# Low-rank products of the decays and rates on 64 rows of the array each, both directions side by side, in place of 128 rows with zeros

## The chip, the cores and the metric

The kernel runs on one core of a Trainium2 chip. A core has five engines with a queue of instructions each: TensorE (PE in the profile, with weight loads as PEld) for matrix products, VectorE (DVE), ScalarE (ACT), GpSimd (POOL) and SyncE (SP), which here issues the transfers between the core's memory and HBM. Each queue runs in order; an instruction waits on semaphores for what it needs. The metric is the device time of one execution in microseconds.

## The reference, cut to what matters

The program is two blocks, one after the other. The first (two layers of sparse attention, convolution and pooling) is not touched. Each of the two layers of the second computes an attention (`_mla`) and a bidirectional recurrence (`_rwkv_bidir`) from one projection, mixes them, and ends with a mixture of experts. The change is in the recurrence, 512 channels wide and 528 positions long, and there in the two products `tanh(wd) @ w2[d]` (decays) and `ad @ a2[d]` (rates), whose inner dimension is 64:

```python
r, k, v, wd_f, wd_b, ad_f, ad_b, gd = _split(u, [RW, RW, RW, 64, 64, 64, 64, 128])
...
def direction(d, wd, ad, reverse):
    wl = w0[d] + jnp.tanh(wd) @ w2[d]
    decay = jnp.exp(-jnp.exp(-jax.nn.softplus(-wl) - 0.5))
    a = jax.nn.sigmoid(a0[d] + ad @ a2[d])
    kd = heads(k * (1.0 + (a - 1.0) * k_a))
    y = _wkv_scan(rh, heads(decay), kd, vh, kk, heads(a), reverse)
    bonus = jnp.sum(rh * kd * r_k, -1, keepdims=True) * vh
    return y, bonus

y_f, bonus_f = direction(0, wd_f, ad_f, False)
y_b, bonus_b = direction(1, wd_b, ad_b, True)
```

## The kernel before, in words

Everything of the second block lies with channels on the 128 partitions and the 528 positions along the free dimension. A product over all positions is made in two halves of 264 (`HALF`), each in a PSUM tile of its own; the pool `ps` has four such tiles. A 32-bit product shows as two matmul instructions in the trace.

`mixers` runs one layer of the second block's first part (about 880 to 1400 us and 1885 to 2400 us of the span). It first makes some projections (`shifted`, which calls `proj_tile`, line 1029). The projections number 12 and 13 are the inputs of the low-rank products: `low[0]` has tanh of the decays' 64 channels of direction 0 in rows 0 to 63 and those of direction 1 in rows 64 to 127; `low[1]` has the same for the rates.

The 512 channels are then worked in four pairs of heads, 128 channels each, by four generators of `rwkv_pair`. `mixers` advances them by turns, by the rules of `RULES`, and between their steps it takes from `fill`, a generator with all other work of the layer: the other projections, the attention, the output. A pair's first steps are named "go", the later ones "invert", "double" and "chain" (short products of 64 columns). In which order instructions then stand on each engine is decided by a scheduler, from the order in which the code issues them and from when tiles come free.

In the "go" steps a pair does the following, first for direction 0 and then for direction 1. It makes the decays (`w0`) and rates (`a0`) with products over `wl` (line 1431, which calls the helper `halves`, line 994); ACT evacuates each half with a tanh (1433); POOL scales the decays (1437); DVE scans them over time (1439 or 1441); POOL, ACT and DVE make the exponentials and the scaled keys from them (1442 to 1456); POOL scales chunks of the keys (1464). Behind the second direction POOL adds the two directions' keys (1469), DVE multiplies that with the receptance (1471), and TensorE sums it over channels for the bonus (1472, again line 994).

The weight tile `wl` (one buffer) has, for each kind and each direction, 128 rows, of which only 64 are filled: the rest is set to zero by POOL (1382), and four transfers (1385) bring 64 rows each. So a product runs over all 128 rows of `low`, and the rows of the other direction meet zeros.

Weights of `fill`'s projections come by transfer (1017) into `big`, and are split into two parts by ACT (932) and POOL (933); `big` has 22 buffers, `u` has 10, and both are shared with `rwkv_pair`.

Of the kernel before, what the change touches and what calls it, by code (L numbers as in the profile page):

```python
# [12 lines left out]
AF = mybir.ActivationFunctionType  # L13
# [9 lines left out]
HALF = 264  # L23
# [169 lines left out]
class K:  # L193
# [1181 lines left out]
    def rwkv_pair(self, l, i, low, v2, vlow, yd):  # L1375

        nc, A = self.nc, self.A
        cs = slice(i * 128, (i + 1) * 128)
        idc = self.c("ident")

        wl = self.t("wl", [128, 2, 2, 128], 1)
        nc.gpsimd.memset(wl, 0.0)
        for j, k in enumerate(("rwkv_w2", "rwkv_a2")):
            for d in range(2):
                nc.sync.dma_start(wl[d * 64:d * 64 + 64, j, d], A[k][l][d * 64:d * 64 + 64, cs])
        rk = self.big()[:, :2 * L2].rearrange("p (j t) -> p j t", j=2)
        nc.sync.dma_start(rk, self.rw[i:i + 5:4].rearrange("j p t -> p j t"))
        R, Kk = rk[:, 0], rk[:, 1]
# [7 lines left out]
        else:  # L1396
            vf, t = self.u()[:, :L2], self.u()[:, :L2]
            nc.sync.dma_start(vf, self.vfirst[i])
            ps = self.halves([v2[:, cs]], [vlow[:32]])
# [7 lines left out]
        s = self.u()[:, :L2]  # L1407
# [6 lines left out]
        kr, bk = [], []  # L1414
# [5 lines left out]
        def chunk(x, o):  # L1420

            if o is None:
                return x[:, :16]
            return x[:, 16:].rearrange("p (c n) -> p c n", n=64)[:, o::2]
        for d in range(2):
            x = self.big().rearrange("p (s n) -> p s n", s=2)
            kr.append(x)
            lw, P = x[:, 0], x[:, 1]
            a, c, kd = self.u()[:, 48:], self.u(), self.u()[:, 48:]
            for j, (dst, nm) in enumerate(((lw[:, 48:], "w0"), (a, "a0"))):  # L1430
                ps = self.halves([wl[:, j, d]], [low[j]])
                for x in range(2):
                    nc.scalar.activation(dst[:, x * HALF:(x + 1) * HALF], ps[x][:, :HALF], AF.Tanh, scale=0.5,
                                         bias=self.pc(nm, d * 4 + i, True))
            yield "go"
            nc.gpsimd.memset(lw[:, :48], 0.0)
            nc.gpsimd.tensor_scalar(lw[:, 48:], lw[:, 48:], e5, e5, op0=ALU.mult, op1=ALU.add)
            if d == 0:
# [16 lines left out]
            x = self.big().rearrange("p (c s n) -> p c s n", c=9, s=2)  # L1455
# [16 lines left out]
        ps = self.halves([self.c("ones64")], [bonus])  # L1472
        for x in range(2):
            xs = slice(x * HALF, (x + 1) * HALF)
# [5 lines left out]
        ps, p8 = self.ps(), self.ps()  # L1480
# [43 lines left out]
        for d in range(2):  # L1524
# [6 lines left out]
            for par in range(2):  # L1531
                both = [self.ps() for _ in range(2)]
                self.warm(both[1])
                for j in range(4):
                    c = 2 * j + par if d == 0 else 8 - 2 * j - par
# [4 lines left out]
                for hh, ps in enumerate(both):  # L1540
# [6 lines left out]
                    for x, G in enumerate((GA, GC)):  # L1547
# [4 lines left out]
            c = 8 if d == 0 else 0  # L1552
            ps = self.ps()
# [3 lines left out]
                             start=True, stop=True)  # L1557
# [15 lines left out]
        for part, k0 in enumerate((0, 3, 6)):  # L1573
            ps = self.ps()
# [830 lines left out]
```

## Time and profile before

| | |
|---|---|
| timed runs | 2747.86, 2748.91, 2754.46 us, median 2748.91 |
| the profiled execution | 2744.74 us, its span 2743.0 us |
| mean granted clock of TensorE | 0.928 of full speed |
| busy: PE, DVE, ACT, POOL | 2368.5, 1490.2, 910.3, 781.8 us |

The span is the time from the first to the last instruction that the profiler shows; the execution's own time is 1.7 us more. Busy times of different engines overlap. A matmul's duration in the trace holds the time until its result is there, so for instructions behind one another the distance of their starts is what each costs.

### The profile page before, as it was taken

Reading aid. Unit: us, or ns where it says so; the run is one execution under the profiler, and the core shown is the slowest. Engines: PE = TensorE matmul, PEld = TensorE weight load, DVE = VectorE, ACT = ScalarE, POOL = GpSimd, SP = SyncE. Lnnn points to the kernel's source line nnn. Section 1 sums busy time; section 2 is a strip of 40 time slices with the busy share of each in tenths; the row PEclk is TensorE's granted clock in tenths of the full one; section 3 lists DMA queues with packets and bytes.
Section 4 is the critical chain, followed back from the end, with each engine's and each line's share of the span. In section 5 each row is a group of like instructions: output and inputs, shape, how many; then the busy total and the mean of one; then the engine's idle time right before and its main releaser. Section 6 shows DMA issues by size and latency. Waiting matters only on the chain. (4 is left out here: it accounts for less than half of the span.)

```text
span 2743.0 us, 48138 instructions
## 1 busy us (share of the span) xinstructions
PE 2368.5 (86%) x19363; PEld 1846.0 (67%) x19363; DVE 1490.2 (54%) x3197; ACT 910.3 (33%) x1832; POOL 781.8 (29%) x707
## 2 busy tenths in 40 slices
PE   8988988987969879988896999779888998969994
PEld 7664887664968767666765666468766677756662
DVE  2896233995246785667536321166766675363213
ACT  3346322246243334445402111143435464021111
POOL 5634425635311640222022110035422120121102
PEclk9998999998989999989998899979899999979997
DMA  5421123411235322101216899663230113179996
GB/s 180 108 70 40 51 79 91 108 54 40 63 128 157 96 89 89 43 22 62 96 65 225 313 416 413 258 206 122 80 101 15 46 65 109 60 263 370 414 409 238
DMA packets 208611, 401.32 MB, mean 146 GB/s; under 512 B 25474, under 2 KB 129538, under 8 KB 197376
## 3 DMA queue, kind: packets, MB, share of 16 engines
q1 hardware_dynamic: 195232, 376.50, 38.7%
q0 software_dynamic: 7776, 14.30, 1.5%
q10 hardware_dynamic: 5376, 7.40, 1.1%
q8 instruction: 154, 2.52, 0.4%
q14 instruction: 73, 0.60, 0.1%
HBM read 351.83 MB, written 52.94 MB: 148 GB/s over the span
## 5 line engine op out<-in xcount | busy, mean ns | idle before, releaser
L294 POOL TENSOR_TENSOR wl<-raw,wh 128x1024 fp32r<-128x1024 f32 (+1 forms) x92 | 220.1, 2402 | 268.5 <-ACT wh L293 268.1
L1029 PE MATMUL sc<-gy,w 128*128 128x264 f32 x1216 | 224.5, 300 | 28.7 <-DVE ph L1900 11.4
L1029 PEld LDWEIGHTS sc<-gy,w 128*128 128x128 f32 x1216 | 183.6, 199 | 38.4 <-issue 13.5
L300 PE MATMUL ps<-wh,xh 128*128 128x256 f32 x640 | 188.1, 294 | 6.3 <-DVE xl L313 3.4
L300 PE MATMUL ps<-wh,xl 128*128 128x256 f32 x640 | 181.1, 283 | 2.5 <-POOL xl L709 2.1
L300 PE MATMUL ps<-wl,xh 128*128 128x256 f32 x640 | 181.4, 284 | 1.1 <-POOL wl L294 1.1
L300 PE MATMUL ps<-xh,wh 128*128 128x512 f32 (+1 forms) x400 | 166.4, 416 | 7.6 <-ACT att L458 7.6
L300 PE MATMUL ps<-xh,wl 128*128 128x512 f32 (+1 forms) x400 | 161.7, 404 | 0.1
L300 PE MATMUL ps<-xl,wh 128*128 128x512 f32 (+1 forms) x400 | 161.7, 404 | 0.0
L2307 PE MATMUL ps<-big,hTr 128*64 128x256 f32 x1200 | 158.8, 384 | 2.6 <-DMA big<-in_moe_w_dram 2.3
L293 ACT ACTIVATE wh<-raw 128x1024 fp32r<-128x1024 f32 (+1 forms) x92 | 93.4, 1029 | 169.6 <-PE ps L300 61.7
L1029 PE MATMUL sc<-big,w 128*128 128x264 f32 x608 | 134.8, 296 | 2.0 <-DVE big L933 2.0
L2307 PEld LDWEIGHTS ps<-big,hTr 128*64 128x64 f32 x1200 | 97.6, 139 | 53.7 <-issue 7.1
L300 PEld LDWEIGHTS ps<-wh,xh 128*128 128x128 f32 x640 | 122.6, 192 | 8.8 <-DVE xl L313 4.0
L526 DVE SCALAR_TENSOR_TENSOR a<-pz,ph,a 128x512 f32<-128x512 f32 x120 | 124.3, 1036 | 2.6
L300 PEld LDWEIGHTS ps<-wh,xl 128*128 128x128 f32 x640 | 122.5, 192 | 3.4 <-POOL xl L709 2.5
L300 PEld LDWEIGHTS ps<-wl,xh 128*128 128x128 f32 x640 | 122.7, 192 | 2.4 <-POOL wl L294 1.4
L2250 DVE SCALAR_TENSOR_TENSOR mh<-mh,ps 128x256 f32<-128x256 f32 x32 | 13.5, 421 | 185.0 <-ACT mh L2249 185.0
L2085 POOL DMA_INDIRECT zd<-my,idx x32 | 31.6, 989 | 271.3 <-ACT my L270 244.5
L1627 ACT ACTIVATE z<-ps,mix 128x512 f32<-128x512 f32 x144 | 77.7, 577 | 80.0 <-PE ps L1517 71.0
L1029 PEld LDWEIGHTS sc<-big,w 128*128 128x128 f32 x608 | 101.9, 199 | 3.2 <-DVE big L933 2.8
L300 PEld LDWEIGHTS ps<-xh,wh 128*128 128x128 f32 (+1 forms) x400 | 77.3, 193 | 36.1 <-ACT att L458 11.3
(497 smaller groups left out, 5896.7 us busy)
## 6 DMA issues: line engine op xcount, KB each, us to landing
big<-in_moe_w_dram SPq DMA_DIRECT2D x216, 512.0 KB
w8m<-in_moe_w_dram SPq DMA_DIRECT2D x48, 1024.0 KB
w<-in_moe_w_dram SPq DMA_DIRECT2D x36, 1024.0 KB
raw<-in_w_in_dram SPq DMA_DIRECT2D x56, 512.0 KB
big<-in_w_in_dram SPq DMA_DIRECT2D x36, 512.0 KB
raw<-in_w_out_dram SPq DMA_DIRECT2D x16, 512.0 KB
raw<-in_ple_gate_w_dram SPq DMA_DIRECT2D x16, 512.0 KB
big<-zd SPq DMA_DIRECT2D x16, 512.0 KB
```

The costliest lines, as they stand in the source:

```text
L293: nc.scalar.activation(hi[:, x:x + 4], v, AF.Copy)
L294: nc.gpsimd.tensor_tensor(lo[:, x:x + 4], v, hi[:, x:x + 4].bitcast(F32), op=ALU.subtract)
L300: self.nc.tensor.matmul(ps, a[x], b[y], start=start and j == 0, stop=stop and j == 2)
L526: nc.vector.scalar_tensor_tensor(acc, u[:, s:s + S], ph[:, tp + s:tp + s + 1], acc, op0=ALU.mult, op1=ALU.add)
L1029: self.nc.tensor.matmul(ps[x][:, :HALF], w[a][:, k], hT[k // 2][b][:, k % 2, x * HALF:(x + 1) * HALF], start=k == 0 and a == b == 0, stop= ...
L1627: nc.scalar.activation(Z[g][q][:, :self.WIDTH[g]], ps[:, :self.WIDTH[g]], AF.Copy, scale=self.c("half")[:, q:q + 1])
L2085: ins = nc.gpsimd.indirect_dma_start(out=zd[:, :], out_offset=bass.IndirectOffsetOnAxis(ap=idx[:, j, 1:2], axis=0), in_=y, in_offset=None, ...
L2250: nc.vector.scalar_tensor_tensor(a, a, 1.0, p1[:, :256], op0=ALU.add, op1=ALU.mult)
L2307: self.nc.tensor.matmul(ps[q * 64:q * 64 + 64, :256], xT[:, k, q * 64:q * 64 + 64], ww[q][k], start=k == 0, stop=k == 7)
```

## The change

`wl` loses its zeros and the dimension for the direction: 128 rows, of which rows 0 to 63 belong to direction 0 and rows 64 to 127 to direction 1. The memset is gone, and one transfer per kind brings both directions. The products of both directions are made in the first "go" step, before any other work on direction 0: for each kind and each half a product over rows 0 to 63 and one over rows 64 to 127, into two PSUM tiles, and then the two evacuations. The tile of direction 1 for the decays (`kr`) and that for the rates (`rates`) are taken in that step too. The number of steps of a pair is the same.

```diff
-        wl = self.t("wl", [128, 2, 2, 128], 1)
-        nc.gpsimd.memset(wl, 0.0)
+        wl = self.t("wl", [128, 2, 128], 1)
         for j, k in enumerate(("rwkv_w2", "rwkv_a2")):
-            for d in range(2):
-                nc.sync.dma_start(wl[d * 64:d * 64 + 64, j, d], A[k][l][d * 64:d * 64 + 64, cs])
+            nc.sync.dma_start(wl[:, j], A[k][l][:, cs])
...
+        rates = []
         for d in range(2):
-            x = self.big().rearrange("p (s n) -> p s n", s=2)
-            kr.append(x)
-            lw, P = x[:, 0], x[:, 1]
-            a, c, kd = self.u()[:, 48:], self.u(), self.u()[:, 48:]
-            for j, (dst, nm) in enumerate(((lw[:, 48:], "w0"), (a, "a0"))):
-                ps = self.halves([wl[:, j, d]], [low[j]])
-                for x in range(2):
-                    nc.scalar.activation(dst[:, x * HALF:(x + 1) * HALF], ps[x][:, :HALF], AF.Tanh, scale=0.5,
+            kr.append(self.big().rearrange("p (s n) -> p s n", s=2))
+            rates.append(self.u()[:, 48:])
+
+        for j, nm in enumerate(("w0", "a0")):
+            for x in range(2):
+                xs = slice(x * HALF, (x + 1) * HALF)
+                ps = [self.ps() for _ in range(2)]
+                for d in range(2):
+                    r = slice(d * 64, d * 64 + 64)
+                    nc.tensor.matmul(ps[d][:, :HALF], wl[r, j], low[j][r, xs], start=True, stop=True)
+                for d in range(2):
+                    nc.scalar.activation((rates[d] if j else kr[d][:, 0, 48:])[:, xs], ps[d][:, :HALF], AF.Tanh, scale=0.5,
                                          bias=self.pc(nm, d * 4 + i, True))
-            yield "go"
+        yield "go"
+        for d in range(2):
+            lw, P = kr[d][:, 0], kr[d][:, 1]
+            a, c, kd = rates[d], self.u(), self.u()[:, 48:]
+            if d:
+                yield "go"
```

Where instructions stand now is shown at three places. Lines of the changed kernel are up to 8 higher there: 1434 and 1436 are the products and their evacuations, 1445 the scaling of the decays (1437 before), 1472 that of chunks of the keys (1464), 1477 the bonus sum (1469).

TensorE, first pair of layer 1, from the last filler matmul (`sc`) ahead of the products (`ps<-u,wl`) on; before:

```order
L1029 MATMUL sc_15999<-gy_15074,w_2655_15897 128x264
L994 MATMUL ps_16063<-u_15358,wl_15958 128x264
L994 MATMUL ps_16064<-u_15358,wl_15958 128x264
L994 MATMUL ps_16069<-u_15547,wl_15958 128x264
L994 MATMUL ps_16070<-u_15547,wl_15958 128x264
L1029 MATMUL sc_16081<-gy_15068,w_2672_15995 128x264
```

and now:

```order
L1434 MATMUL ps_16048<-u_15346,wl_15946 128x264
L1434 MATMUL ps_16049<-u_15346,wl_15946 128x264
L1434 MATMUL ps_16054<-u_15346,wl_15946 128x264
L1434 MATMUL ps_16055<-u_15346,wl_15946 128x264
L1029 MATMUL sc_16078<-gy_15056,w_2672_15980 128x264
L1029 MATMUL sc_16079<-gy_15056,w_2672_15980 128x264
L1029 MATMUL sc_16078<-big_15057,w_2672_15980 128x264
L1029 MATMUL sc_16079<-big_15057,w_2672_15980 128x264
L1029 MATMUL sc_16078<-gy_15056,w_2672_15980 128x264
L1434 MATMUL ps_16060<-u_15535,wl_15946 128x264
L1434 MATMUL ps_16061<-u_15535,wl_15946 128x264
L1434 MATMUL ps_16066<-u_15535,wl_15946 128x264
```

The four products of direction 0 have become four of both directions' decays, and the four of the rates (one more stands behind the rows shown) follow five filler products later; the four of direction 1 that stood a hundred matmuls further on are gone from there.

ACT at the same place (evacuations of the products, then the splits of the filler's weights, `w<-big`); before:

```order
L1433 ACTIVATE big_16059<-ps_16063,ph_2562_15078 128x264
L1433 ACTIVATE big_16059<-ps_16064,ph_2562_15078 128x264
L1433 ACTIVATE u_16060<-ps_16069,ph_2562_15078 128x264
L1433 ACTIVATE u_16060<-ps_16070,ph_2562_15078 128x264
L932 ACTIVATE w_2688_16077<-big_16075 128x1024
L932 ACTIVATE w_2694_16158<-big_16156 128x1024
```

and now:

```order
L1436 ACTIVATE big_16044<-ps_16048,ph_2562_15066 128x264
L1436 ACTIVATE big_16046<-ps_16049,ph_2562_15066 128x264
L1436 ACTIVATE big_16044<-ps_16054,ph_2562_15066 128x264
L1436 ACTIVATE big_16046<-ps_16055,ph_2562_15066 128x264
L1436 ACTIVATE u_16045<-ps_16060,ph_2562_15066 128x264
L1436 ACTIVATE u_16047<-ps_16061,ph_2562_15066 128x264
L1436 ACTIVATE u_16045<-ps_16066,ph_2562_15066 128x264
L1436 ACTIVATE u_16047<-ps_16067,ph_2562_15066 128x264
L932 ACTIVATE w_2692_16074<-big_16072 128x1024
L932 ACTIVATE w_2700_16157<-big_16155 128x1024
```

Eight evacuations stand ahead of the two splits now, where there were four.

POOL, later in the same pair, up to the bonus sum (1469 before, 1477 now) and the weight split (933) behind it; before:

```order
L1437 TENSOR_SCALAR big_16215<-big_16215 128x528
L1382 MEMSET wl_16380 128x512
L933 TENSOR_TENSOR w_2707_16233<-big_16231,w_2707_16233 128x1024
L1393 MEMSET big_16388 128x48
L933 TENSOR_TENSOR w_2713_16315<-big_16313,w_2713_16315 128x1024
L1442 TENSOR_TENSOR big_16215<-u_16217,big_16215 128x576
L1447 TENSOR_TENSOR u_16218<-u_16218,big_15964 128x528
L1453 TENSOR_TENSOR big_16215<-big_15964,big_16215 128x528
L1454 MEMSET big_16215 128x2x48
L1469 TENSOR_TENSOR u_16062<-u_16062,u_16218 128x528
L1464 TENSOR_TENSOR big_16304<-u_16218,u_16217 128x16
L1464 TENSOR_TENSOR big_16304<-u_16218,u_16217 128x4x64 x2
```

and now:

```order
L1444 MEMSET big_16481 128x48
L933 TENSOR_TENSOR w_2713_16300<-big_16298,w_2713_16300 128x1024
L1450 TENSOR_TENSOR big_16046<-u_16214,big_16046 128x576
L933 TENSOR_TENSOR w_2731_16399<-big_16397,w_2731_16399 128x1024
L1455 TENSOR_TENSOR u_16215<-u_16215,big_15949 128x528
L1461 TENSOR_TENSOR big_16046<-big_15949,big_16046 128x528
L1462 MEMSET big_16046 128x2x48
L1472 TENSOR_TENSOR big_16289<-u_16215,u_16214 128x16
L1472 TENSOR_TENSOR big_16289<-u_16215,u_16214 128x4x64 x2
L1477 TENSOR_TENSOR u_16132<-u_16132,u_16215 128x528
```

The bonus sum has moved behind the three scalings of the second direction, one more weight split (`w_2731`, which stood behind it) is ahead of it, and the scaling of the second direction's decays and the memset of `wl` are no longer here.

## Rows read from the trace of the kernel before

**Rows 1.** Part 1 of the page: busy us, share of the span, instructions.

```profile
PE 2368.5 (86%) x19363; PEld 1846.0 (67%) x19363; DVE 1490.2 (54%) x3197; ACT 910.3 (33%) x1832; POOL 781.8 (29%) x707
```

**Rows 2.** Windows: length, busy PE, PEld, DVE, ACT, POOL; PEclk; DMA; GB/s.

```profile
880.00:1400.00 520.00, 455.09 (x4964) 362.56 (x4963) 344.04 (x790) 223.92 (x451) 144.96 (x151) 0.93 0.24 77
1885.00:2400.00 515.00, 454.50 (x4883) 366.26 (x4882) 329.20 (x760) 206.23 (x417) 135.09 (x151) 0.94 0.22 72
```

**Rows 3.** Work on `wl`; durations in ns as least/median/most, first and last start.

```profile
L994 PE MATMUL ps<-u,wl x128: 383/386/490, 884.7 to 2214.0; 128*128 128x264 f32 x128
...
L1385 SPq DMA_DIRECT2D wl<-in_rwkv_w_dram x16: 471/588/1882, 816.8 to 2110.1; - x16
...
L1382 POOL MEMSET wl<- x8: 519/522/527, 813.9 to 2109.0; 128x512 f32 x8
```

**Rows 4.** Timeline, TensorE: start, us, engine, line, tiles, rows*columns, form, count.

```profile
1885.25 1.94 PE L994 MATMUL ps<-u,wl 128*128 128x264 f32 x8
```

**Rows 5.** Timeline, TensorE, two places of the first block with 64-row matmuls.

```profile
142.88 0.39 PE L300 MATMUL ps<-xl,wh 128*128 128x512 f32 x1
143.11 0.40 PE L300 MATMUL ps<-xh,wl 128*128 128x512 f32 x1
143.44 0.49 PE L642 MATMUL pq<-a,a 64*128 64x128 f32 x4
143.86 0.50 PE L300 MATMUL ps<-xh,wh 128*128 128x512 f32 x1
...
184.57 0.70 PE L642 MATMUL pq<-a,a 64*128 64x256 f32 x4
185.20 0.50 PE L300 MATMUL ps<-xh,wh 128*128 128x512 f32 x1
```

**Rows 6.** Timeline, TensorE, a product among the chain's short ones.

```profile
1089.00 0.71 PE L994 MATMUL ps<-u,wl 128*128 128x264 f32 x2
```

**Rows 7.** Timeline, ACT, first pair of layer 1 (idle before in brackets).

```profile
1885.89 0.93 ACT L1433 ACTIVATE big<-ps,ph 128x264 f32<-128x264 f32 x2 [0.17 <-PE ps L994]
...
1887.61 1.99 ACT L932 ACTIVATE w<-big 128x1024 fp32r<-128x1024 f32 x2
...
1899.62 0.93 ACT L1433 ACTIVATE big<-ps,ph 128x264 f32<-128x264 f32 x2 [0.17 <-PE ps L994]
```

**Rows 8.** Timeline, DVE and TensorE, end of that pair's first steps.

```profile
1916.26 0.75 DVE L1471 SCALAR_TENSOR_TENSOR u<-u,pv,big 128x528 f32<-128x528 f32 x1
...
1917.07 1.25 PE L994 MATMUL ps<-u,mix 128*128 128x264 f32 x2 [4.06 <-DVE u L1471]
```

**Rows 9.** Timeline, POOL, the same pair.

```profile
1888.74 5.41 POOL L933 TENSOR_TENSOR w<-big,w 128x1024 fp32r<-128x1024 f32 x2 [0.97 <-ACT w L932]
...
1901.42 0.62 POOL L1437 TENSOR_SCALAR big<-big 128x528 f32<-128x528 f32 x1
...
1907.00 2.38 POOL L933 TENSOR_TENSOR w<-big,w 128x1024 fp32r<-128x1024 f32 x1 [1.29 <-ACT w L932]
...
1914.61 1.44 POOL L1469 TENSOR_TENSOR u<-u,u 128x528 f32<-128x528 f32 x1
1916.01 2.46 POOL L1464 TENSOR_TENSOR big<-u,u 128x16 f32<-128x16 f32 x3
```

**Rows 10.** Timeline, POOL and TensorE, second pair of layer 0.

```profile
967.32 0.78 POOL L1437 TENSOR_SCALAR big<-big 128x528 f32<-128x528 f32 x1 [1.56 <-ACT big L1433]
...
971.04 1.43 POOL L1442 TENSOR_TENSOR big<-u,big 128x576 f32<-128x576 f32 x1 [2.48 <-DVE u L1441]
...
978.31 2.68 POOL L933 TENSOR_TENSOR w<-big,w 128x1024 fp32r<-128x1024 f32 x1
...
965.47 2.14 PE L994 MATMUL ps<-u,wl 128*128 128x264 f32 x8
...
981.05 0.92 PE L1029 MATMUL sc<-gy,w 128*128 128x264 f32 x4 [3.65 <-POOL w L933]
```

**Rows 11.** Timeline, TensorE, second pair of layer 1.

```profile
1977.98 2.00 PE L994 MATMUL ps<-u,const 128*128 128x264 f32 x4 [4.38 <-ACT u L1089]
```

## The prediction

> **What bounds the kernel now.** I read the page's busy times first, then the busy time by stage, then all work on the tile of the low-rank weights, then the timelines of the places where the products stand. TensorE is busy for 86% of the span and everything else for about half or less [rows 1]. The page's chain of the end cannot be used here (it stops at the last few instructions), so what bounds a place is read from the waits on TensorE there. In the two stretches in which the changed code runs (about 880 to 1400 us and 1885 to 2400 us), TensorE is also busy for some 88% of the time [rows 2]. The idle rest is not one wait but many of 1 to 4 us, where a chain of POOL, ACT and DVE work or a weight transfer comes late. A saving on TensorE is worth its full size only where TensorE runs without gaps up to the next wait. Where it already waits, the saving turns into more waiting, and what counts is how the change moves POOL and ACT.
>
> **The products on TensorE.** There are 64 products (four per direction, half and kind: 8 pairs times 8), each of two instructions, so 128 [rows 3]. Eight in a row take 1.94 us with the last one's 0.386 us of latency [rows 3, 4]: (1.94 - 0.386) / 7 = 0.222 us from start to start, 0.444 us a product, and 64 x 0.444 = 28.4 us in all. After the change a product uses rows 0 to 63 or rows 64 to 127 of the array. Whether two such run side by side is shown by the scores of the first block, which have the same form (64 rows, 128 columns): four instructions of 256 columns, two products, start at 184.57 and are over at 185.20, so 0.63 us, where one after the other at 0.222 x 256/264 = 0.215 us they would take 0.86 [rows 5]. They do overlap, but two streams are 0.43, so 0.20 us more is spent inside the group. Its neighbours pay as well: the full-row matmul ahead of a group of such products holds TensorE for 0.33 us (143.11 to 143.44) where the same kind took 0.23 just before, and the one behind it takes 0.50 us where its kind takes 0.40 [rows 5]. So going into the 64-row form and out again costs 0.20 + 0.10 + 0.10 = 0.4 us, 0.2 us a change of form. The same shows on these very products, where two stand alone among products of another form: two instructions take 0.71 us, not 0.386 + 0.222 = 0.61 [rows 6].
>
> What follows for groups of different size: one pair of products alone between full-row work costs 0.444 + 0.4 = 0.84 us against 0.89 before, so nothing is won. Two pairs in a row cost 0.89 + 0.4 = 1.29 against 1.78.
>
> The Trainium skill (TensorEngine Tiling (Array Packing), Key Properties) says "Mode switching requires drain", which speaks against this change; the trace agrees, with the 0.1 us on either neighbour. The Trainium skill (TensorE: Matmul & The Clock Gate, Part 3: Packing small matmuls) gives a pack of such tiles the time of one matmul plus about 4 ns for each further one. By it all 32 pairs would halve, 14.2 us; by the trace's 0.2 us a change of form the sum is the smaller one that follows.
>
> In the order of the changed kernel, 27 times the two products of a pair of directions stand behind one another, and 10 products stand alone, since their two accumulators did not come free together. So 37 streams are left of 64: 37 x 0.444 = 16.4 us, 12.0 us less. Over TensorE's whole order, changes of form go from 953 to 972. Next to the products there are about 35 more; 16 fewer elsewhere come from other work standing in another order. 19 x 0.2 = 3.8 us. The most that TensorE's own work can shrink is therefore 12.0 - 3.8 = 8.2 us. If the fewer changes elsewhere are worth nothing, it is 12.0 - 7.0 = 5.0 us.
>
> **The other edits.** The memset goes: 8 x 0.52 = 4.2 us of POOL; and 16 of the 32 small transfers, 0.59 us of SP each, 9.4 us in all [rows 3]. POOL is busy for 29% and SP waits on buffers, so both are worth nothing by themselves except where POOL is the chain that is waited for (the first pairs, below). The 64 evacuations on ACT stay, 0.93 us for two [rows 7]. But all eight of a pair now come in one go, where four came early and four some 14 us later. A tile of `big` and one of `u` per pair are held longer; both pools (22 and 10 buffers) are shared with the weights of the filler work, so weights may be fetched one tile later. I take nothing for this, since the order of the fetches changes by one place only; were it a transfer late, it is one wait like the 3.65 us of [rows 10].
>
> **First pair of layer 1 (1885 to 1921 us).** Here TensorE has filler work up to about 1913 and then waits 4.06 us for the bonus, the DVE product at 1916.26 [rows 8]. DVE waits for POOL's sum at 1914.61, and POOL works through its queue almost without a gap from 1888.74 on [rows 9]. That queue sets the end, and the change makes it longer. First, ACT does eight evacuations ahead of the two weight splits instead of four, 4 x 0.46 = 1.9 us later [rows 7], and POOL's first split then starts some 1.7 us later. Then POOL's order: the bonus sum (old line 1469) now stands behind its direction's three scalings instead of ahead of them (2.46 us) and behind one more weight split (2.38 us). Against this, the rescaling of the second direction moves ahead of the splits (-0.62), the memset is gone (-0.52), and a wait of 1.29 us for a weight split on ACT is filled [rows 9]. Sum: 1.7 + 2.46 + 2.38 - 0.62 - 0.52 - 1.29 = +4.1 us. I take +4. The bounds: without the late start and with all of the wait gone it is +2.4; with the wait still there +5.4. TensorE's 0.5 to 1 us saved ahead of this place only lengthens its wait. The weight split that is pulled ahead may spare a later wait, which could give one or two of these back.
>
> **First pair of layer 0 (884 to 925 us).** The same chain ends in the same wait. It was shorter there and the added split does not stand in the way: the later ACT work (+1.9) less the memset (-0.52) and idle POOL time like the 0.97 us of [rows 9] leaves +0.5 us (0 to +1.9).
>
> **Second pairs.** In layer 0 TensorE waits 3.65 us for a weight split on POOL, which starts at 978.31 [rows 10]. POOL stood idle twice ahead of it, 1.56 us for the evacuations of direction 1 and 2.48 us for the scan behind them, and those hang on the four products at 965.47. These products now stand right behind those of the first direction, some 30 us earlier, so both idles can go; the split on ACT, which waits for its transfer, allows only part. I take -1.5 us (0 to -2.4). In layer 1 the matmuls of this pair stand ahead of a wait of 4.38 us for attention data [rows 11], which does not come earlier: -0.5 us. After such a wait TensorE's instructions also run slower for a while (four take 2.00 us at 1977.98 [rows 11], eight 1.94 in [rows 4]), so each microsecond of wait that goes or comes has some tenths with it.
>
> **Third and fourth pairs.** These lie in the chain stages, where TensorE has short products of 64 columns. Their streams shrink from 32 to 19 slots, 13 x 0.444 = 5.8 us, and about 11 changes of form more take 2.2 us back: 3.6 us. TensorE is busy there for much the same share as in the whole [rows 2] and waits in many small pieces, so I let some 70% pass: -2.5 us (0 to -3.6).
>
> **Sum.** +4 + 0.5 - 1.5 - 0.5 - 2.5 = 0.0 us. The profiled execution took 2744.74 us; the median of the timed runs is 2748.91, 4.2 us above it. I predict no change that can be measured: 2748 us on the scale of the median, with the little that other reordered work may give. A change under 0.3%, 8.2 us, can't be told from none here.
>
> **Rivals.**
> *The saving on TensorE passes in full.* For it: TensorE is the busy engine [rows 1, 2], and weight splits pulled ahead can fill gaps. The 8.2 us are then all kept, the second pairs give 2 us, and the bonus chain costs nothing in the end, since the pulled-ahead split removes a later wait of the same size: -10 us, and with the quicker running behind shorter waits up to -12, about 2737 us. Against it: waits stand behind the products in four of the eight pairs. Chance 0.27. The packing rule of the Trainium skill (TensorE: Matmul & The Clock Gate, Part 3) would put it a few us lower still.
>
> *ACT's eight evacuations in one go hold up what is behind them (slower).* The price is 1.9 us at each of 8 pairs [rows 7], 15 us, if the instruction behind them on ACT is one that TensorE waits for: weight splits in the first two pairs, evacuations of the chain in the other two. POOL's order in the first pair of layer 1 adds 2.4 us (4.1 less its late start). With half or all of the 8.2 us saved this gives +9 to +14, about 2759 us. With half saved it can be measured from 1.9 n + 2.4 - 4.1 = 8.2 on, n = 5 to 6 pairs of eight. Against it: ACT is busy for a third only. Chance 0.14.
>
> *The halves do not run side by side here*, because the two accumulators come free at different times or the two weights have to be loaded in turn. Then no stream is saved, 3.8 to 7 us of changes of form and the 4 us of the first pair come on top: +8 to +11, about 2758 us. Against it stands the overlap of 0.63 us in [rows 5], with the same form. Chance 0.06.
>
> No change: 0.53, by itself 2742 to 2755. The range that holds eight in ten reaches to the rivals on both sides: 2737 to 2758 us. Faster 0.27, same 0.53, slower 0.20.
>
> **What would show it.** Right: pairs of the new products start within about 0.01 us of each other and eight instructions end within 1.3 us; busy TensorE falls by 5 to 8 us; the wait ahead of the bonus in the first pair of layer 1 grows from 4.06 to about 8 us; the one for the weight split in the second pair of layer 0 falls to 2 us or less; windows from 1000 to 1400 and 2065 to 2300 us hold the same work 1 to 2 us earlier each. Wrong: starts 0.22 us apart; a wait of several us in the chain stages that ends on an ACT evacuation; weights fetched later; or a gain in stretches that the change does not touch, through the order.

## The result, and the profile after

The changed kernel is slower: 2765.76 us (2756.23 to 2771.45, six runs) against 2749.03 us of the kernel before (six runs), a ratio of 1.0062 with an interval of 1.0046 to 1.0079. I had predicted 2748 us with a range up to 2758. Its profiled execution took 2771.45 us at a granted clock of 0.921.

Part 1 of the page of the changed kernel answers to [rows 1], the two windows (same columns) to [rows 2]:

```profile
PE 2378.4 (86%) x19363; PEld 1844.7 (67%) x19363; DVE 1499.7 (54%) x3197; ACT 911.2 (33%) x1834; POOL 776.0 (28%) x699
```

```profile
880.00:1400.00 520.00, 452.37 (x4898) 359.73 (x4896) 338.62 (x776) 222.04 (x448) 138.45 (x147) 0.91 0.24 76
1885.00:2400.00 515.00, 440.16 (x4806) 350.76 (x4806) 337.10 (x756) 212.80 (x427) 132.47 (x148) 0.92 0.23 74
```

In the window of layer 1 TensorE was busy for 454.50 us and is busy for 440.16 now, with 77 matmuls fewer done by its end: so it waits more there, and is not held by longer work. Over the whole span its busy time rose from 2368.5 to 2378.4 us, where I had expected 5 to 8 us less; these durations hold the lower granted clock too, 0.921 against 0.928. The work on the weight tile, which answers to [rows 3]:

```profile
L1434 PE MATMUL ps<-u,wl x128: 382/383/806, 882.1 to 2209.8; 64*128 64x264 f32 x128
...
L1383 SPq DMA_DIRECT2D wl<-in_rwkv_w_dram x8: 333/358/1967, 816.1 to 2111.6; - x8
L1383 SPq DMA_DIRECT2D wl<-in_rwkv_a_dram x8: 413/430/738, 816.6 to 2112.0; - x8
```

And the products of the first pair of layer 1 on TensorE (timeline; [rows 4] is the same place before):

```profile
1895.26 1.16 PE L1434 MATMUL ps<-u,wl 64*128 64x264 f32 x8
1896.35 0.51 PE L1029 MATMUL sc<-gy,w 128*128 128x264 f32 x2
1896.69 0.41 PE L1029 MATMUL sc<-big,w 128*128 128x264 f32 x2
```

Eight take 1.16 us in place of 1.94, their starts are 7 ns apart within a pair of directions, and the filler behind them takes 0.51 us where it otherwise takes 0.41. So the halves run side by side here and the prices of the form are near those of the prediction. The Trainium skill (TensorE: Matmul & The Clock Gate, Part 3: Packing small matmuls) has about 4 ns for each further tile of a pack; the trace agrees in kind, with 7 ns, but shows the 0.1 us on the neighbour as well.

**Where the time went.** For each matmul I took its start in a trace less the start of the same matmul in the trace of before. The table gives this distance (us, + is later), the median over the matmuls that start in the 20 us from the given time of before on; "again" are second executions, "place only" is an experiment below:

```
time in before             860  1060  1180  1300  1860  1960  2060  2180  2300  2700
changed                   -2.7   0.9   3.8   7.9   9.9  13.4  14.5  17.8  23.5  25.6
changed, again            -1.9   1.1   4.0   8.0  10.1  13.6  14.5  17.8  23.5  21.6
place only, full rows     -3.2   0.0   3.2   6.6   6.3   9.4   9.6  13.7  18.6  20.3
before, again             -3.0  -6.0  -6.0  -4.4  -2.7  -6.6  -6.0  -6.1  -7.0  -9.0
```

Between 860 and 1060 stand the first and second pairs of layer 0, up to 1180 the third, up to 1300 the fourth; likewise for layer 1 up to 2060, 2180 and 2300. The last line shows what two executions of one kernel differ by: 3 to 4 us in the stages of the first pairs, 1.6 or less in those of the third and fourth. The third and fourth pairs lose 2.9 and 4.1 us in layer 0, 3.3 and 5.6 in layer 1, 15.9 us together (from distances before rounding), and the second execution repeats each within 0.1. The first two pairs lose 3.6 and 4.6 us, which the table alone could not tell from chance; the wait that is shown under e7 tells it for layer 1.

Two limits of this table. The two profiled executions lie 26.7 us apart and the medians 16.7, so its stages add up to more than the ratio says. And two executions of the kernel before are few: in the trace of e3 below, where the third and fourth pairs have the code of before, the distance goes from 0.7 at 1180 to 7.9 at 1300. There the granted clock (the eighth column) is low; e3, then the kernel before:

```profile
1300.00:1310.00 10.00, 10.00 (x84) 6.48 (x86) 5.91 (x17) 0.73 (x2) 2.12 (x1) 0.52 0.26 84
```

```profile
1300.00:1310.00 10.00, 9.86 (x170) 9.06 (x167) 7.75 (x28) 5.34 (x14) 0.00 (x0) 1.00 0.26 79
```

So a difference like the 4.1 us of the fourth pair of layer 0 can arise without the change, though the changed order repeats it; in the other three stages e3 has 0.1 us or less.

### The profile page after: what moved, and what is told of

It is laid out like the page before. It is cut to its first block, busy times and chain, and to the rows that moved or that the text cites. A ratio compares the mean times of both kernels' runs of the same rounds, so it can differ in the third digit from the quotient of the medians.

```text
span 2769.7 us, 48112 instructions
## 1 busy us (share of the span) xinstructions
PE 2378.4 (86%) x19363; PEld 1844.7 (67%) x19363; DVE 1499.7 (54%) x3197; ACT 911.2 (33%) x1834; POOL 776.0 (28%) x699
## 5 line engine op out<-in xcount | busy, mean ns | idle before, releaser
L1715 ACT ACTIVATE w<-ps 64x256 f32<-64x256 f32 x64 | 24.1, 377 | 251.4 <-PE ps L1706 239.9
```

Source lines behind the costliest of these rows:

```text
L1715: nc.scalar.activation(UV[qs, s].rearrange("p d n -> p (d n)"), pu[qs, :256], AF.Copy, scale=-1.0)
```

## The experiments

Ratios are to the kernel before on the same chip, with 95% intervals; each distance is to the trace of before, as in the table.

**e1: the rows alone.** The old order, and products over 64 rows one direction after the other.

```diff
-        wl = self.t("wl", [128, 2, 2, 128], 1)
-        nc.gpsimd.memset(wl, 0.0)
+        wl = self.t("wl", [128, 2, 128], 1)
...
-                ps = self.halves([wl[:, j, d]], [low[j]])
+                r = slice(d * 64, d * 64 + 64)
+                ps = self.halves([wl[r, j]], [low[j][r]])
```

> The products use 64 rows each (no zeros, no memset, one transfer per kind), but stay where they stood before, four per direction, so that none runs beside another; the order on TensorE and ACT is that of the kernel before. If the lost time comes from the form (43 changes of form more, 0.2 us each, nothing saved): 5 to 9 us slower than before. If it comes from where the products and their evacuations stand: within 4 us of before.

2759.61 us against 2747.68, 1.0037 (1.0022 to 1.0053), with TensorE and ACT in the same order as before. So the form by itself, with nothing side by side, costs 10 us by the ratio, 12 by the medians. It is not spread over the 64 products: up to 1200 us the distance is 0.4, and at 1220 it is 7.8. This place comes back under e15 and e14.

**e2: the place alone.** The changed order, with full rows and zeros as before.

```diff
-                    r = slice(d * 64, d * 64 + 64)
-                    nc.tensor.matmul(ps[d][:, :HALF], wl[r, j], low[j][r, xs], start=True, stop=True)
+                    nc.tensor.matmul(ps[d][:, :HALF], wl[:, j, d], low[j][:, xs], start=True, stop=True)
```

> The products keep 128 rows with zeros, but those of both directions are made in the first step, in the order of the change; the order on ACT is that of the changed kernel, and on TensorE too. If the place is the cause: as slow as the changed kernel or more, 15 to 24 us over the kernel before, since the 12 us of streams that run side by side are missing. If the form is the cause: within 4 us of before.

2763.69 us, 1.0064 (1.0046 to 1.0082): all of the loss, with no 64-row product in the kernel. Its line in the table loses 3.2, 3.4, 4.1 and 4.9 us in the third and fourth pairs, 15.6 together. The place is the main cause. What the form gains and costs inside this order cancels, within the intervals. Nor is it the granted clock: the mean of e2's runs is 0.925, that of the runs of the kernel before beside them 0.924.

**e3 and e4: the change for the first two pairs of each layer alone, and for the last two alone** (`i < 2` or `i >= 2` chooses the new code, otherwise the old).

> The whole change for the first two pairs of each layer only, the other two as before. If the time is lost in the chain stages of pairs three and four (15 of the 25 us that the two traces lie apart): 4 to 9 us slower than before, most of it in the first pair of layer 1, whose bonus chain comes 4 us later. If the loss is spread over all pairs alike: 8 to 9 us.

> The whole change for the third and fourth pairs of each layer only. If the time is lost in the chain stages: 8 to 16 us slower than before, and the first pairs run as before. If it was lost by what the first pairs shift: within 4 us of before, or faster by the 3 us of streams that run side by side.

2755.23 us, 1.0024 (1.0008 to 1.004), and 2758.48 us, 1.0039 (1.0021 to 1.0056): 7.6 and 10.8 us, which add up to about the whole. Both halves of the change lose, by the medians the last two pairs more (the intervals overlap), where I had expected a gain of 2.5 us. The trace of e3 has +2.6 us in the first two pairs of layer 0 and +4.4 in those of layer 1, near the changed kernel's.

**e5: the tile of direction 1 taken late.** As the changed kernel, but direction 1's tile of `big` is taken only at its turn; its decays are evacuated into a tile of `u` until then.

```diff
-            kr.append(self.big().rearrange("p (s n) -> p s n", s=2))
+            if d == 0:
+                kr.append(self.big().rearrange("p (s n) -> p s n", s=2))
             rates.append(self.u()[:, 48:])
+        dec = [kr[0][:, 0, 48:], self.u()[:, 48:]]
...
             if d:
                 yield "go"
+                kr.append(self.big().rearrange("p (s n) -> p s n", s=2))
```

> The changed kernel, but the decays of direction 1 are evacuated into a small tile (u), and the big tile for them is taken only when direction 1 is worked, as before. If the lost time in the third pair of layer 0 is the wait of that evacuation for a big buffer, which the earlier pair's chain gives up at its end: the attention's exponentials stand ahead of the rest of the chain on ACT again, the chain's steps there are filled with other work, and 3 to 6 us of the 18 come back. If it is only the eight evacuations in one go: within 2 us of the changed kernel.

It was aimed at this row of waits in the changed kernel, on ACT in the third pair of layer 0 (timeline; [idle before and what ended it]):

```profile
1090.16 0.48 ACT L1436 ACTIVATE big<-ps,ph 128x264 f32<-128x264 f32 x1 [0.26 <-PE ps L1434]
1093.29 0.38 ACT L1715 ACTIVATE w<-ps 64x256 f32<-64x256 f32 x1 [2.65 <-PE ps L1706]
1096.88 0.38 ACT L1715 ACTIVATE w<-ps 64x256 f32<-64x256 f32 x1 [3.21 <-PE ps L1706]
...
1107.69 0.38 ACT L1715 ACTIVATE w<-ps 64x256 f32<-64x256 f32 x1 [3.27 <-PE ps L1706]
1108.50 0.85 ACT L1436 ACTIVATE big<-ps,ph 128x264 f32<-128x264 f32 x2 [0.44 <-PE ps L1718]
1109.78 0.85 ACT L1436 ACTIVATE u<-ps,ph 128x264 f32<-128x264 f32 x2 [0.43 <-PE ps L1434]
1110.53 0.68 ACT L1174 ACTIVATE u<-sc,sm 128x512 f32<-128x512 f32 x1
```

The evacuation at 1108.50 waits not for its product but for line 1718, a chain matmul of another pair, which reads a tile of `big`. I take it for the last reader of the tile into which direction 1's decays go; the trace does not name the buffer, and e5 tries it. In ACT's order the evacuation stands behind the steps of that chain. Until the chain ends, ACT does only these, 3.2 us idle before each; behind the evacuation stands the attention (line 1174, at 1110.53). In the kernel before it ran at 1090.25, and in e5 at 1089.92:

```profile
1090.25 0.69 ACT L1174 ACTIVATE u<-sc,sm 128x512 f32<-128x512 f32 x1
```

```profile
1089.92 0.68 ACT L1174 ACTIVATE u<-sc,sm 128x512 f32<-128x512 f32 x1
```

In the changed kernel TensorE so has no attention to fill the chain with either; e2, with full rows, has the same wait at 1107.68 and the attention at 1109.79. The same 30 us of the changed kernel, of e5 and of the kernel before (windows, columns as in [rows 2]):

```profile
1080.00:1110.00 30.00, 24.41 (x323) 19.93 (x323) 12.70 (x36) 7.54 (x19) 3.03 (x9) 0.93 0.01 1
```

```profile
1080.00:1110.00 30.00, 29.27 (x399) 22.43 (x397) 17.07 (x38) 14.67 (x34) 5.02 (x8) 0.99 0.02 6
```

```profile
1080.00:1110.00 30.00, 29.84 (x381) 23.71 (x382) 18.27 (x50) 15.00 (x38) 5.27 (x8) 0.94 0.06 20
```

With the tile taken late TensorE is busy for 29.27 of 30 us again, and the distance goes from -2.0 at 1080 to -1.8 at 1140 where the changed kernel's goes from 0.8 to 4.2. At its place the cause is shown. The whole kernel does not show it: 2764.14 us, 1.0073 (1.0054 to 1.0091), at a lower granted clock (mean of its runs 0.921, of the changed kernel's 0.924). The two intervals are too wide to tell some 3 us from nothing, so whether the gain reached the end or was lost again elsewhere is not shown.

**e7: the bonus sum first.** As the changed kernel, with POOL's sum of the two directions ahead of the second direction's three scalings.

```diff
             iP = c[:, 48:]
+            if d == 0:
+                bonus = kd
+            else:
+                nc.gpsimd.tensor_tensor(bonus, bonus, kd, op=ALU.add)
             for o, q in ((None, 1), (0, 0), (1, 1)):
```

> The changed kernel, with the sum for the bonus written ahead of the second direction's three scalings; every other engine's order stays. By the price of the prediction the first pair of layer 1 gets 2.46 us back, and up to 2 us more in the other pairs: 2 to 4 us faster than the changed kernel. If the bonus is not what sets the end there: no difference.

The place it is about, in the changed kernel: POOL, DVE and TensorE (timelines), first pair of layer 1, against [rows 8, 9].

```profile
1897.32 1.77 POOL L1445 TENSOR_SCALAR big<-big 128x528 f32<-128x528 f32 x2 [15.74 <-ACT big L1436]
...
1900.53 2.39 POOL L933 TENSOR_TENSOR w<-big,w 128x1024 fp32r<-128x1024 f32 x1 [1.33 <-ACT w L932]
1903.90 2.40 POOL L933 TENSOR_TENSOR w<-big,w 128x1024 fp32r<-128x1024 f32 x1 [0.98 <-ACT w L932]
...
1927.33 1.64 POOL L1472 TENSOR_TENSOR big<-u,u 128x16 f32<-128x16 f32 x3
1928.93 1.29 POOL L1477 TENSOR_TENSOR u<-u,u 128x528 f32<-128x528 f32 x1
```

```profile
1930.26 0.77 DVE L1479 SCALAR_TENSOR_TENSOR u<-u,pv,big 128x528 f32<-128x528 f32 x1 [2.73 <-POOL u L1477]
```

```profile
1921.75 0.40 PE L1029 MATMUL sc<-gy,w 128*128 128x264 f32 x2
1931.08 1.25 PE L994 MATMUL ps<-u,mix 128*128 128x264 f32 x2 [8.93 <-DVE u L1479]
```

TensorE's wait for the bonus has grown from 4.06 to 8.93 us: this is the +4 of the prediction, with POOL busy from 1903.90 to 1930 and the sum last in its queue. In e7 the distance grows from 9.6 to 12.1 us over this wait (1900 to 1920), in the changed kernel from 9.3 to 14.1: 2.3 us are given back, priced at 2.46 [rows 9]. But the whole is 2770.12 us, 1.0086 (1.0067 to 1.0106), no faster than the changed kernel. Between 1960 and 1980 the distance grows by 3.3 us, in the changed kernel by 0.6. What is won at a wait here need not reach the end.

**e9: e5 and e7 together.**

> Both of the edits before: the late big tile and the earlier bonus sum. If both causes are real and lie in different places, their gains add: 5 to 9 us faster than the changed kernel, still 9 to 13 us slower than the kernel before.

2760.95 us, 1.0053 (1.0034 to 1.0072). That is 16.5 us by medians over the kernel before on its chip, where the changed kernel is 16.7 over it: a gain of 5 to 9 us over the changed kernel does not show, and it is still clearly slower than before. Against e7 alone, on the same chip, it is 9 us faster.

**e10: half of the products later.** The decays of both directions in the first step, the rates of both right behind the next "go" (`products(0, "w0")`, `yield "go"`, `products(1, "a0")`).

> The changed kernel, but only the decays of both directions are made in the first step, and the rates of both at the start of the second, so that four evacuations come in one go and not eight. If the eight in one go hold up ACT: 4 to 8 us faster than the changed kernel. If the big tile of direction 1 is the cause: no faster, since it is taken as early as in the changed kernel.

2786.38 us, 1.0153 (1.0133 to 1.0173): 42 us, more than twice the change itself. Moving half of the products back by a step does not halve the loss.

**e11, e13 and e12: how early?** The kernel before with full rows; direction 1's four products are issued in another step of direction 0 (e11: the third, one step early; e13: the second, two early; the change is three early), or its decays alone in the first (e12).

```diff
+        products(0, (0, 1))
         for d in range(2):
...
+            if d == 0:
+                products(1, (0, 1))
             nc.vector.tensor_copy(Pe[:, :, d], P[:, 63::64] if d == 0 else P[:, 512::-64])
```

> The kernel before (128 rows with zeros), with the four products of direction 1 and their evacuations issued one step earlier than before, in the third step of direction 0 (the change has them three steps earlier). If what costs time is how early they are made (buffers and ACT's queue taken from the chain of the earlier pair): 0 to 6 us slower than before, less than two steps, and that less than the 18 us of three steps. If any other order than the tuned one costs as much: 10 us or more already here.

> The same with the four products of direction 1 two steps earlier, in the second step of direction 0. By the theory of earliness 6 to 12 us slower than before, between one step and three. By the theory of any other order: no trend with the number of steps.

> The kernel before, with only the two products of direction 1's decays in the first step (three steps early, with the big tile), those of its rates where they were. If the big tile taken early is the larger part: 8 us or more slower than before. If it is the number of evacuations in one go (six instead of eight, against four): about half of the 18 us.

One step early: 2749.57 us, 1.0011 (0.9997 to 1.0025), no difference that can be told. Two: 2778.51 us, 1.0116 (1.0096 to 1.0135). Three (e2): 1.0064. The decays of direction 1 alone, three early: 2754.77 us, 1.0026 (1.001 to 1.0041). The price is not proportional to how early the products stand or to how long the tiles are held; each place gives another order, with its own waits. Why two steps cost more than three is not settled.

**e14: both kinds side by side, in the old place.** Rows 0 to 63 of `low[d]` hold direction d's decays and rows 64 to 127 its rates (columns of the projection's weights change places), so a direction's own two products fill the array, at the step where they stood before.

```diff
+            for x in range(2):
+                xs = slice(x * HALF, (x + 1) * HALF)
+                ps = [self.ps() for _ in range(2)]
+                for j in range(2):
+                    r = slice(j * 64, j * 64 + 64)
+                    nc.tensor.matmul(ps[j][:, :HALF], wl[r, d], low[d][r, xs], start=True, stop=True)
```

> A version that keeps each direction's products where the kernel before has them and still lets two run side by side: the columns of two projections are laid out anew, so that a direction's decays and rates (not the two directions) lie in rows 0 to 63 and 64 to 127, and a direction's four products are two pairs. By the prices found, 27 of 32 pairs stand together (12 us of streams less) and there are 45 changes of form more (9 us): 3 us faster than the kernel before at most, 0 to 3 if the waits around take it up. If any change of the order costs as much as the ones measured so far: 5 us or more slower.

2751.44 us, 1.0025 (1.0012 to 1.0038). Without the move most of the loss is gone, but a little remains, with fewer streams on TensorE.

**e15, e16 and e17: second profiled executions** of e1, of the kernel before and of the changed one, for the place at 1200 us.

> A second profile of the kernel with 64 rows in the old places. If the low granted clock from 1200 to 1240 us belongs to this form: it is low there again and some 7 us are lost at that place. If it comes and goes: it stands elsewhere or nowhere, and the place costs 1 us or less, as the changes of form alone would.

> A second profile of the kernel before. If the low stretches come and go: this profile has some in other places than the first, and its time differs from the first's by what they cost (the runs of this kernel spread from 2738 to 2758 us).

> A second profile of the changed kernel. The waits that follow from the order (first pair of layer 1, third pair of layer 0, third and fourth of layer 1) are the same within 0.5 us each; what differs from the first profile by more stands where the granted clock differs.

One execution each: 2753.25, 2735.57 and 2767.28 us, with another run of the kernel before at 2746.69 alongside. The granted clock behind the fourth pair's products of layer 0 (the eighth column): the kernel before, then e1.

```profile
1210.00:1220.00 10.00, 9.06 (x103) 7.23 (x103) 8.65 (x20) 4.45 (x9) 3.68 (x5) 1.00 0.01 2
```

```profile
1210.00:1220.00 10.00, 9.79 (x62) 7.56 (x64) 5.60 (x16) 1.86 (x5) 1.46 (x2) 0.52 0.01 2
1220.00:1230.00 10.00, 10.00 (x85) 8.25 (x82) 5.14 (x12) 4.51 (x11) 3.04 (x4) 0.50 0.01 2
```

In e1 the clock stands at its lower level of 1.2 GHz here, 62 matmuls are done in 10 us in place of 103, and this is where its 7.4 us go. The second executions repeat it: e16 has 1.00 in both windows, e15 has 0.50 and 0.62, and its distance goes from -2.4 at 1180 to 8.4 at 1300, more than its whole loss. The kernel before has such a stretch too, at 1190 to 1200 (0.50), but none behind these products. e4, with 64 rows there as well, in the changed order, has one:

```profile
1210.00:1220.00 10.00, 8.45 (x52) 4.95 (x50) 6.95 (x17) 4.29 (x11) 4.36 (x5) 0.65 0.01 2
1220.00:1230.00 10.00, 10.00 (x78) 8.71 (x79) 3.79 (x14) 4.33 (x11) 2.16 (x3) 0.50 0.00 1
```

**e18, e19 and e20: the form by pairs.** As e14, with side-by-side products in the first three pairs, in the first two, or in none (the others over full rows with zeros). TensorE, ACT and DVE have the same order in all four kernels.

```diff
+        side = i < 2
```

> As the kernel with decays and rates side by side, at the same order, but the fourth pair of each layer has full rows with zeros. If the 64-row products bring the low granted clock there: the clock from 1200 to 1220 us is high again, and it is 5 to 10 us faster than with all four pairs side by side, that is 0 to 4 us faster than the kernel before. If the low clock belongs to the order: no faster than with all four.

> The same, with the third pair on full rows too: only the first two pairs of each layer run side by side. If the form costs in the chain stages and gains among filler work: about as fast as with three pairs, within 3 us.

> The same order, with full rows and zeros in all pairs: the form of the kernel before, with the projections' columns in the new layout. If what the order does is small here: within 3 us of the kernel before, and the first two pairs side by side are 1 to 3 us faster than this. If the order is what costs 6 us: as slow as the kernel with all pairs side by side.

e18 2746.52 us, 0.9999 (0.9985 to 1.0014); e19 2741.95 us, 0.9982 (0.9971 to 0.9992); e20 2744.13 us, 0.9994 (0.9982 to 1.0005). By medians the form in the first two pairs is worth 2.2 us (intervals overlap), in the third it costs 4.6, in the fourth 4.9 (e14, on another chip). The price of the third is one of the medians alone: in e18's trace the distance to e20 is -3.1 us at 1060 and -3.3 at 1160. e19 is faster than both kernels, than the one before by 0.2%. In e14, then in e18, TensorE at the fourth pair (timelines), and the window that holds what follows:

```profile
1198.68 1.25 PE L1436 MATMUL ps<-u,wl 64*128 64x264 f32 x4 [0.70 <-DVE big L1570]
1200.46 2.83 PE L1583 MATMUL ps<-d,mix 128*128 128x72 f32 x12
```

```profile
1200.00:1210.00 10.00, 10.00 (x66) 8.41 (x66) 4.41 (x11) 3.04 (x7) 3.50 (x4) 0.50 0.01 2
```

```profile
1202.94 1.13 PE L1439 MATMUL ps<-u,wl 128*128 128x264 f32 x4 [0.69 <-DVE big L1573]
1204.19 1.56 PE L1586 MATMUL ps<-d,mix 128*128 128x72 f32 x12
```

```profile
1200.00:1210.00 10.00, 8.71 (x90) 7.02 (x90) 9.27 (x22) 4.59 (x11) 4.68 (x5) 1.00 0.01 3
```

The same twelve matmuls take 2.83 us behind 64-row products and 1.56 behind full rows. Against e20, e14 is 7.6 us ahead at 1160 and 4.9 us behind at 1220; over the same stretch e18 loses 1.9 and e19 1.6 us.

## Why the prediction was wrong

**The step that failed is "Third and fourth pairs", -2.5 us.** I priced streams and changes of form on TensorE, 3.6 us, and let 70% pass. Measured: 7.0 us later in layer 0 and 8.9 in layer 1, and with full rows in the same order (e2) 6.6 and 9.0. By medians e4, the change in these pairs alone, is 10.8 us slower than before. So the sign came from the order, not from TensorE's work. Nor was that work as I counted it: I had 13 times two products side by side in these pairs, and of their 26 second instructions only 12 start within 0.02 us of their partner. The sentence that hid the order is "A tile of `big` and one of `u` per pair are held longer", with "I take nothing for this" behind it. I had thought of holding a tile too long; the price lay in asking for it too early. The evacuation then stands behind a chain of another pair that frees the tile, and the attention that would have filled the chain stands behind the evacuation, at 1110.53 in place of 1090.25. This is shown for the third pair of layer 0 by e5, some 3 us of the 15.9. For the other three stages the cause stays open, and only a part was traced: in the third pair of layer 1 a wait for a transfer is 5.19 us, where its kind had 3.36 before (TensorE, the kernel before, then the changed one):

```profile
2124.62 1.83 PE L1198 MATMUL sc<-u,u 128*128 128x128 f32 x8 [3.36 <-DMA u<-vd]
```

```profile
2141.66 2.08 PE L1198 MATMUL sc<-u,u 128*128 128x128 f32 x8 [5.19 <-DMA u<-vd]
```

**The first pair of layer 1, +4: right**, by the mechanism as put: wait 4.06 to 8.93 us, 4.8 us later over it, of which e7 gives back the 2.3 us that stand for the bonus sum's place.

**The first pair of layer 0 and the second pairs, +0.5, -1.5, -0.5: wrong, in size at least.** Layer 0's two pairs give +3.6 where I had -1.0; a part of it may be chance. The 3.65 us wait did not fall: TensorE waits 4.83 us at this place, now for DVE. POOL and TensorE of the changed kernel (timelines) against [rows 10]:

```profile
971.25 1.43 POOL L1450 TENSOR_TENSOR big<-u,big 128x576 f32<-128x576 f32 x1 [5.66 <-DVE u L1449]
...
978.20 2.70 POOL L933 TENSOR_TENSOR w<-big,w 128x1024 fp32r<-128x1024 f32 x1
```

```profile
981.37 0.59 PE L1029 MATMUL sc<-gy,w 128*128 128x264 f32 x1 [4.83 <-DVE u L1039]
```

The two idles of POOL that I wanted to remove became one of 5.66 us, which ends on DVE's scan; the split starts at 978.20 where it started at 978.31. DVE was late there, not the products that I had moved.

**The prices of the form: right locally, incomplete as a sum.** Eight products take 1.16 us and the neighbour pays 0.1. Of the 54 second instructions in the 27 pairs, 37 start within 0.02 us of their partner. What 0.2 us a change of form leaves out is the granted clock: in the old place the same form brought 7.4 us of 1.2 GHz behind one group of products (e1). In the changed kernel this place stands at 0.70 to 0.81 (1200 to 1220), and in e2 with full rows at 0.83 to 0.86; in that order the form costs as much as it saves, since e2 and the changed kernel take the same time within their intervals.

**The rivals.** That ACT's evacuations hold up what is behind them had 0.14 and the nearest time, 2759 us, by another price: where it was traced, not 0.46 us for each of four more evacuations, but one evacuation that stands 18 us behind the one before it, for want of a tile. That the halves do not run side by side is refuted by the 37 starts within 0.02 us, and that the saving passes in full by the total.

**What stays open.** Which waits make up the fourth pairs' losses and the third's in layer 1; why two steps early cost more than three; and why the totals of e5 and e7 do not show what their places had won. Their runs stand at a lower clock (0.921, the kernel before beside them 0.924), and over some 220 runs of all kernels here, each against the mean of its own kernel, 0.001 of mean clock goes with 1.5 us, so 0.003 goes with some 5 (an estimate from these runs); but whether the clock is the cause or only goes with the waits, no run tells.

## What to carry to other kernels

When an edit issues work earlier, list the tiles that it asks for and who frees them. What stands behind a late evacuation in its engine's queue is the price, as the attention did here; engine time saved says nothing of it. Put two half-array products side by side where they are already neighbours (here the two kinds of one direction, in the pairs whose filler is of full size), and try form and place as separate kernels: here the place cost 16 us, and the form was by medians worth 2 in the first two pairs and cost 5 in the third pairs and 5 in the fourth.

## What was not expected of the hardware

- Behind the 64-row products of the fourth pair of layer 0, among the chain's short matmuls, the granted clock stood at 0.50 to 0.65 for some 20 us in four traces of three kernels (e1 twice, e14, e4). With full rows five traces (before twice, e18, e19, e20) had 1.00 there, and four (e2, e3, e11, e12) 0.83 to 0.85 for 10 us and then 1.00. In e1 that costs about 7 us. It is this place and not the form everywhere: behind the 64-row products of the third pairs and of layer 1's fourth pair, e1 has, over 20 us, the clock of the kernel before within 0.02. Why here is open.
- Two executions of one kernel differ by 9 us (2744.74 and 2735.57) at the same mean clock of 0.928, 3 to 4 us of it in each layer's first two pairs, and a third trace has 7 us in a stage whose code is the same (e3). A difference smaller than that cannot be read from a stage of a single trace.
